# Weight blocks in fours, dots five gathers behind, and a yield between one-hots and their matmuls

## The chip, the cores and the metric

The kernel runs on one core of one Trainium2 chip. The metric is the time of one launch in microseconds on the device. Before the change three runs took 3744.71, 3747.1 and 3749.22 us; the median is 3747.1 us.

## What is computed

One layer of a decoder in float32 for two groups of rows: a prompt of 1024 rows (eight tiles of 128 rows, t = 0 to 7) and a sample group of 64 rows (tile 8, half a tile). Cut to what matters here:

```
h  = x @ w_in                                   # 1024 -> 3072, six chunks of 512 columns
a  = gelu(ua) * spatial_gate(gelu(va))          # two chunks
r  = silu(gr) * LN(retention(rot(q), rot(k), v))# four chunks, state carried from tile to tile
x1 = LN(ALPHA * x  + concat(a, r) @ w_o)
x2 = LN(ALPHA * x1 + attention(x1 @ ca_wq, mem_k, mem_v) @ ca_wo)
q  = x2 @ peer_wq                               # four chunks, 8 heads x 2 halves x 128
s  = q . subkeys;  top-16 per half -> 256 sums -> top-16 -> softmax weights g, expert numbers e
y  = LN(ALPHA * x2 + sum_e g_e * gelu(U[e] . x2) * V[e])     # 128 experts of 16384 per row
```

The results are y, the memory keys and values, the retention states and the normalised gate rows of the sample group.

## The kernel before

**Two streams.** Python generators emit the program: `main()` (the front, then the dense part) and `gathers()`. A loop at the end of `body` (L1154) advances the one whose clock is behind. Every `yield` names a cost, which is added to that stream's clock, and the clock is the due time (`tc.cur_priority`) of what is emitted next. Before the run a planner lays out each engine's queue: it walks through a modelled timeline and gives a free engine the earliest-due instruction that is ready in that model. On the chip each queue then runs strictly in that order, and an instruction whose input is late holds up all behind it.

**Front.** The tiles go through in four batches, [0], [1, 2, 8], [3, 4, 5], [6, 7]. `plan` lists chunks (a batch, a weight matrix and 512 of its columns): six of `w_in`, two each of `w_o`, `wq`, `wo`, and then four of `pq`, which for batches 1 and 2 are spread between the next batch's `w_in` chunks. A chunk has KB = 8 weight blocks of 128x512 (256 KB each), which SP loads in order into NR = 9 buffers (`Weights.load`, L136); a block's buffer is free once the last tile of the batch has used it. `Weights.mm` (L144) multiplies one tile by GK blocks in a row. The loop at L834 goes over KB / GK groups of blocks and, inside, over the tiles:

```
for grp in range(KB // GK):
    for t in tiles:
        ...
        yield from W.mm(i, grp, p[:P], lhs(key, t), lt)
        if grp < KB // GK - 1:
            step_all()
            continue
```

Each tile's sum is in one of three PSUM buffers (`mm`). After its last group, a tile's follow-up work (`post_gate`, `post_ret`, `post_att`, `post_res`, `post_peer`) joins the list `active`; each `step_all()` moves every entry one piece further. With the first chunk of `w_o`, `wq`, `wo` and `pq`, `drain(t)` first runs tile t's follow-up work to its end.

**Experts by gathers.** Tiles 0, 8, 5, 6 and 7 get their experts by indirect DMAs from the POOL queue: 576 gathers of 512 KB from U and as many from V into a ring of NG = 7 buffers (`gbuf`). `jobs` lists them in the order u0 v0 u8 v8 u5 v5 and so on. For each U gather `use` (L1062) emits one DVE instruction, the dot at L1071 with the rows of x2, due 15 units (DO) later than its place and put behind the DVE instruction emitted just before (`pin`). For each four V gathers PE does sixteen small matmuls (`cb`, L1104). A job is used LAG = 3 jobs after its gather is emitted. One job costs 1.1 units in the front; two weight blocks of a tile cost 1.3.

**Experts by tables.** Tiles 1 to 4 go through the dense part, which multiplies with all of U and V and needs a table of weights by expert. The end of `post_peer` builds it, one tile at a time (`gsl`): three transposes (L691), then for each of 32 groups g of four rows the one-hots (ACT at L702 and L703, DVE at L705), four matmuls (L719), an ACT copy into `big` (L720) and, for each four groups, a DMA to `gsc` (L723). One-hots for group g + 1 are emitted ahead of the matmuls of group g; the generator yields after every second group. The dense part waits for all four tables: `while st.get("gsl") or ...` (L988), and its own buffers open only when those of the tables are closed (L1000).

**Dense part.** 128 steps of `do_h` (L968) and of the V matmuls (L1024), with the rest of the gathers beside them.

Of the kernel before, what the change touches and what calls it, by code (L numbers as in the profile page):

```python
# [18 lines left out]
NT = 8  # L19
SMP = 8  # L20
KB = 8
GK = 2
ALPHA = 2.0 ** 0.25
EPS = 1e-5
GAM = [1.0 - 2.0 ** (-5.0 - h) for h in range(4)]
# [39 lines left out]
NG = 7  # L65
VQ = 4
LAG = 3
NFL = 3
ND = 2
GT = [0,8,5,6,7]  # L70
# [88 lines left out]
def body(ctx: ExitStack, tc: tile.TileContext, a):  # L159
    nc = tc.nc  # L160
# [94 lines left out]
    done = {}  # L255
# [332 lines left out]
    def post_peer(t, c, p, sub):  # L588
        P = rows(t)
# [95 lines left out]
        if c == 3 and dn:  # L685
            while st.get("gsl") or not st.get("gok"):
                yield
            st["gsl"] = True
            tp = GB()
            for j, src in enumerate((eid[:, 0, :], eid[:, 1, :], gw)):  # L690
                nc.tensor.transpose(tp[:, j * 128:(j + 1) * 128], src, ident)  # L691
            kt = TQ([128, 5, 128], "kt", 1)
            tpv = tp[:, :384].rearrange("p (a b) -> p a b", a=3)
            nc.scalar.activation(kt[:, :3, :], tpv, AF.Copy)
            nc.scalar.activation(kt[:, 3:5, :], tpv[:, 1:3, :], AF.Copy, scale=-1.0)
            yield
            n = DT.index(t)

            def onehots(g):
                oj = TQ([128, 4, 128], "oj", OJ)  # L700
                for r in range(4 * g, 4 * g + 4):
                    nc.scalar.activation(oj[:, r % 4, :], iota, AF.Abs, bias=kt[:, 3, r:r + 1])  # L702
                    nc.scalar.activation(oj[:, r % 4, :], oj[:, r % 4, :], AF.Relu, bias=kt[:, 2, r:r + 1], scale=kt[:, 4, r:r + 1])  # L703
                oi = TQ([128, 4, 128], "oi", OI)
                x = nc.vector.tensor_tensor(oi, iota.unsqueeze(1).to_broadcast([128, 4, 128]),  # L705
                                            kt[:, 0, 4 * g:4 * g + 4].unsqueeze(2).to_broadcast([128, 4, 128]), op=ALU.is_equal)
                pin(x, PO)
                return oi, oj

            nxt = onehots(0)  # L710
            for g in range(32):
                if g % 4 == 0:
                    gs = TQ([128, 128, 16], "big")
                oi, oj = nxt
                if g < 31:
                    nxt = onehots(g + 1)
                g4 = GB()
                for r in range(4):
                    nc.tensor.matmul(g4[:, r * 128:(r + 1) * 128], lhsT=oj[:, r, :], rhs=oi[:, r, :], start=True, stop=True)  # L719
                nc.scalar.activation(gs[:, :, g % 4 * 4:g % 4 * 4 + 4].rearrange("p i t -> p t i"),  # L720
                                     g4.rearrange("p (t i) -> p t i", t=4), AF.Copy)
                if g % 4 == 3:
                    nc.sync.dma_start(gsc[8 * n + g // 4], gs)  # L723
                if g % 2:
                    yield
            st["gsl"] = False
        elif c == 3:
            tp = GB() if XG else SM()
            nc.tensor.transpose(tp[:, :P], eid[:P, 0, :], ident[:P, :P])
            nc.vector.tensor_copy(done["ixT", t][:, :P], tp[:, :P])  # L730
            done["v", t] = True
            if t == SMP:
                for x in (done["ix", t], gw):
                    nc.sync.dma_start(x[64:, :64], x[:64, 64:])
                done["u", t, 3] = True
# [57 lines left out]
    def front():  # L793
        for i, (bi, name, c) in enumerate(plan):
# [39 lines left out]
            for grp in range(KB // GK):  # L834
                for t in tiles:
# [9 lines left out]
                        ps[t] = MM()  # L845
                    p = ps[t]
                    lt = t == tiles[-1]
                    yield from W.mm(i, grp, p[:P], lhs(key, t), lt)
                    if grp < KB // GK - 1:
                        step_all()  # L850
                        continue
                    del ps[t]
                    if c == NCH[name] - 1 and name != "wk":
# [196 lines left out]
    def gathers():  # L1050
# [75 lines left out]
                    nc.sync.dma_start(lb, bc(a["ln3_b"], 1024))  # L1126
                    finish(y, t, lg, lb)

        for m in range(len(jobs) + LAG):
            if m < len(jobs):  # L1130
                kind, t, i = jobs[m]
                P = rows(t)
                need = ("v", t) if kind == "v" else ("u", t, 3 if t == SMP else i // 32)
                while need not in done:
                    yield None
                if kind == "u" and i == 0:
                    x2s[t] = TG([128, 1024], "x2g", 1)
                    for j in range(0, 128, P):
                        nc.sync.dma_start(x2s[t][j:j + P], done["x2", t])
                g = TG([128, 1024], "gbuf", NG)  # L1140
                bufs[m] = g
                if kind == "u":
                    nc.gpsimd.indirect_dma_start(out=g, out_offset=None, in_=a["U"],  # L1143
                                                 in_offset=bass.IndirectOffsetOnAxis(ap=done["ix", t][:, i:i + 1], axis=0))
                else:
                    nc.gpsimd.indirect_dma_start(out=g, out_offset=None, in_=a["V"],  # L1146
                                                 in_offset=bass.IndirectOffsetOnAxis(ap=done["ixT", t][:, i:i + 1], axis=0))
            if m >= LAG:
                use(m - LAG)
            yield COST_F if phase[0] == 0 else COST_G  # L1150

    clocks = {"f": 0.0, "g": 0.0}
# [74 lines left out]
```

## Time and profile before

| | |
|---|---|
| runs | 3744.71, 3747.1, 3749.22 us; median 3747.1 |
| profiled execution | 3735.99 us, span 3734.1 us |
| PE | 3311.8 us busy (89%), mean granted clock 0.930 |
| DVE / ACT / POOL | 2331.6 (62%) / 1284.7 (34%) / 1573.6 us (42%) |
| DMA | 1039.72 MB, mean 278 GB/s |

All numbers come from one profiled execution. "Busy" is the time in which an engine ran an instruction; the granted clock is a share of TensorE's full 2.4 GHz. A float32 matmul of the program stands as two records in the trace. Idle time before an instruction is put down to the engine or DMA that released it.

### The profile page before, as it was taken

What the parts mean: (1) busy time and instruction counts of PE and PEld (TensorE: products, weight loads), DVE (VectorE), ACT (ScalarE), POOL (GpSimd) and SP (SyncE); (2) the same over time, 40 slices, a digit from 0 to 9 for tenths busy, and PEclk for the clock granted to TensorE, in tenths of its full rate; (3) what the DMA queues carried; (4) which work ended last, traced back from release to release, by engine and by line L of the source; (5) the groups of instructions that cost most, each with busy time, mean ns of one, the idle gap of its engine ahead of it and who ended that gap; (6) DMA issues with size and microseconds to landing.
All of it is one profiled execution on the core that took longest, in us unless ns stands there. A gap on an engine that the chain in (4) does not pass through costs nothing.

```text
span 3734.1 us, 42405 instructions
## 1 busy us (share of the span) xinstructions
PE 3311.8 (89%) x13881; PEld 2052.1 (55%) x13881; DVE 2331.6 (62%) x5894; ACT 1284.7 (34%) x2642; POOL 1573.6 (42%) x1363
## 2 busy tenths in 40 slices
PE   8999467889987999955888699999999999999998
PEld 3443223333445554432544477777777777666786
DVE  2135873225778523899759488788777777544556
ACT  1121211112258884222778722222222222222222
POOL 0013674244547532456645355454455544434100
PEclk9989688889988999977998799999999999999999
DMA  8757578677769886757988799999999999888632
GB/s 279 241 171 263 205 298 315 227 278 270 276 209 367 304 307 239 278 197 251 338 308 308 277 334 334 323 327 332 321 329 337 326 325 321 308 312 310 215 102 73
DMA packets 407356, 1039.72 MB, mean 278 GB/s; under 512 B 37280, under 2 KB 129632, under 8 KB 403040
## 3 DMA queue, kind: packets, MB, share of 16 engines
q0 software_dynamic: 165888, 604.05, 44.8%
q1 hardware_dynamic: 229392, 420.06, 32.9%
q10 hardware_dynamic: 11856, 12.91, 1.0%
q8 instruction: 109, 1.79, 0.2%
q14 instruction: 111, 0.91, 0.1%
HBM read 985.59 MB, written 51.25 MB: 278 GB/s over the span
## 4 chain that ended last, share of the span: by engine, by line
PE 63%; DVE 13%; DMA 11%; issue 5%; POOL 4%; ACT 4%; SPq 0%; POOLq 0%; ACTq 0%; DVEq 0%
PE mm L148 19%; PE h L973 15%; PE cb L1104 6%; PE oa L1024 4%; PE ob L1024 4%; PE oc L1024 4%; PE od L1024 4%; DVE gbuf L1071 4%; DMA gbuf<-in_V_dram,ixT 4%; DMA gbuf<-in_U_dram,ix 3%; PE gb L719 2%; POOL gbuf L1143 2%; DMA ret<-in_cv_dram 1%; PE sm L296 1%; POOL gbuf L1146 1%
## 5 line engine op out<-in xcount | busy, mean ns | idle before, releaser
L148 PE MATMUL mm<-wr,aT 128*128 128x512 f32 (+1 forms) x2432 | 1125.6, 610 | 31.1 <-DMA aT<-in_xpT_dram 17.9
L1146 POOL DMA_INDIRECT gbuf<-in_V_dram,ixT x576 | 619.0, 1075 | 838.5 <-PE cb L1104 495.5
L1143 POOL DMA_INDIRECT gbuf<-in_U_dram,ix x576 | 719.8, 1250 | 587.0 <-DVE hd L1071 349.1
L1071 DVE CUSTOM_DVE_ANT_0 gbuf<-gbuf,x2g 128x1024 f32<-128x1024 f32 x576 | 707.6, 1242 | 242.9 <-DMA gbuf<-in_U_dram,ix 199.0
L148 PEld LDWEIGHTS mm<-wr,aT 128*128 128x128 f32 (+1 forms) x2432 | 439.1, 190 | 583.3 <-issue 538.5
L973 PE MATMUL h<-x,uh 128*128 128x512 f32 x2048 | 644.2, 393 | 1.0 <-ACT uh L917 1.0
L973 PEld LDWEIGHTS h<-x,uh 128*128 128x128 f32 x2048 | 385.1, 189 | 105.4 <-issue 19.3
L973 PE MATMUL h<-x,ul 128*128 128x512 f32 x1024 | 402.1, 393 | 3.3 <-DVE ul L918 3.3
L1104 PE MATMUL cb<-gbuf,Z 128*32 128x512 f32 x2304 | 300.9, 621 | 25.7 <-DMA gbuf<-in_V_dram,ixT 25.7
L917 ACT ACTIVATE vh<-vr 128x1024 fp32r<-128x1024 f32 x128 | 135.5, 1061 | 546.0 <-PE od L1024 538.0
L719 PE MATMUL gb<-oi,oj 128*128 128x128 f32 x1024 | 170.7, 315 | 68.3 <-ACT big L720 37.5
L719 PEld LDWEIGHTS gb<-oi,oj 128*128 128x128 f32 x1024 | 153.2, 220 | 125.5 <-ACT oj L703 44.1
L973 PEld LDWEIGHTS h<-x,ul 128*128 128x128 f32 x1024 | 193.1, 189 | 52.3 <-issue 6.7
L918 DVE TENSOR_TENSOR ul<-ur,uh 128x1024 fp32r<-128x1024 f32 x128 | 156.5, 1222 | 95.4 <-ACT uh L917 95.1
L703 ACT ACTIVATE oj<-oj,kt 128x128 f32<-128x128 f32 x512 | 215.5, 485 | 0.0
L917 ACT ACTIVATE uh<-ur 128x1024 fp32r<-128x1024 f32 x128 | 135.4, 1059 | 231.2 <-PE h L973 227.3
L917 ACT ACTIVATE ah<-ga 128x512 fp32r<-128x512 f32 x128 | 80.8, 632 | 354.4 <-DVE ga L980 335.7
L705 DVE TENSOR_TENSOR oi<-cst,kt 128x512 f32<-128x512 f32 x128 | 88.9, 700 | 125.7 <-PE gb L719 124.4
L702 ACT ACTIVATE oj<-cst,kt 128x128 f32<-128x128 f32 x512 | 161.6, 391 | 14.8 <-PE gb L719 14.6
L660 POOL TENSOR_TENSOR cd<-cd,sif 128x512 f32<-128x512 f32 (+1 forms) x72 | 104.5, 1465 | 145.5 <-DVE cd L658 137.6
L1104 PEld LDWEIGHTS cb<-gbuf,Z 128*32 128x32 f32 x2304 | 62.5, 111 | 176.3 <-issue 138.4
L918 DVE TENSOR_TENSOR vl<-vr,vh 128x1024 fp32r<-128x1024 f32 x128 | 155.7, 1218 | 3.2 <-ACT vh L917 3.1
(228 smaller groups left out, 4796.7 us busy)
## 6 DMA issues: line engine op xcount, KB each, us to landing
ur<-in_Ud_dram SPq DMA_DIRECT2D x128, 512.0 KB, 6.6
vr<-in_V_dram SPq DMA_DIRECT2D x128, 512.0 KB, 5.8
wr<-in_w_in_dram SPq DMA_DIRECT2D x192, 256.0 KB, 5.3
wr<-in_pq_dram SPq DMA_DIRECT2D x128, 256.0 KB, 5.2
gsc<-big SPq DMA_DIRECT2D x32, 1024.0 KB, 6.8
G<-gsc SPq DMA_DIRECT2D x32, 1024.0 KB, 17.1
wr<-in_w_o_dram SPq DMA_DIRECT2D x64, 256.0 KB, 5.4
wr<-in_wq_dram SPq DMA_DIRECT2D x64, 256.0 KB, 7.4
```

What stands on the lines that cost most here:

```text
L148: self.nc.tensor.matmul(p, lhsT=lT(k), rhs=w, start=k == 0, stop=k == KB - 1)
L702: nc.scalar.activation(oj[:, r % 4, :], iota, AF.Abs, bias=kt[:, 3, r:r + 1])
L703: nc.scalar.activation(oj[:, r % 4, :], oj[:, r % 4, :], AF.Relu, bias=kt[:, 2, r:r + 1], scale=kt[:, 4, r:r + 1])
L719: nc.tensor.matmul(g4[:, r * 128:(r + 1) * 128], lhsT=oj[:, r, :], rhs=oi[:, r, :], start=True, stop=True)
L917: nc.scalar.activation(hi, raw, AF.Copy)
L918: nc.vector.tensor_tensor(lo, raw, hi.bitcast(F32), op=ALU.subtract)
L973: nc.tensor.matmul(p, lhsT=w[:, k, :], rhs=x[:, k, :], start=k == 0 and j == 0, stop=k == 7 and j == 2)
L1024: nc.tensor.matmul(o[j], lhsT=A[i][ia][:, n * 128:(n + 1) * 128], rhs=Vw[i][iv][:, j * 512:(j + 1) * 512], start=b == 0 and ia + iv == 0, ...
L1071: dot = nc.vector.tensor_tensor_reduce(out=g, in0=g, in1=x2s[t], scale=1.0, scalar=0.0, op0=ALU.mult, op1=ALU.add, accum_out=hd[t][:, i:i ...
L1104: nc.tensor.matmul(comb[t][q:q + 32, :], lhsT=Z[:, z + 4 * c1 + r1 % 4, 31 - r1:63 - r1], rhs=g1[:, n * 512:(n + 1) * 512], start=r1 == VQ ...
L1143: nc.gpsimd.indirect_dma_start(out=g, out_offset=None, in_=a["U"], in_offset=bass.IndirectOffsetOnAxis(ap=done["ix", t][:, i:i + 1], axis=0))
L1146: nc.gpsimd.indirect_dma_start(out=g, out_offset=None, in_=a["V"], in_offset=bass.IndirectOffsetOnAxis(ap=done["ixT", t][:, i:i + 1], axis=0))
```

## The change

GK goes from 2 to 4: a tile uses four blocks in a row, and a chunk has two groups instead of four. `step_all()` is still called after every two blocks except the last two of a chunk, so a chunk has as many as before. In `post_peer` the generator now yields in every group, between the one-hots of g + 1 and the matmuls of g: 32 yields instead of 16. In `gathers`, a U job is used five jobs behind (LAGU) while the stream is inside a run of U jobs with no V job pending and no final rows held; otherwise three behind as before. At the first U job of a tile all earlier jobs are used first. V jobs keep their lag. NG, NR and the work itself stay as they are.

```diff
-GK = 2
+GK = 4
+LAGU = 5
...
                 if g < 31:
                     nxt = onehots(g + 1)
+                yield
                 g4 = GB()
...
                 if g % 4 == 3:
                     nc.sync.dma_start(gsc[8 * n + g // 4], gs)
-                if g % 2:
-                    yield
...
-                    yield from W.mm(i, grp, p[:P], lhs(key, t), lt)
+                    for n, cost in enumerate(W.mm(i, grp, p[:P], lhs(key, t), lt)):
+                        yield cost
+                        if n < GK // 2 - 1 or grp < KB // GK - 1:
+                            step_all()
                     if grp < KB // GK - 1:
-                        step_all()
                         continue
...
-        for m in range(len(jobs) + LAG):
+        used = 0
+        for m in range(len(jobs) + 1):
...
                 if kind == "u" and i == 0:
+                    while used < m:
+                        use(used)
+                        used += 1
                     x2s[t] = TG([128, 1024], "x2g", 1)
...
+                del g
-            if m >= LAG:
-                use(m - LAG)
+            while used < m and (m == len(jobs) or m - used >= (LAGU if jobs[used][0] == kind == "u" and not pend and not fl else LAG)):
+                use(used)
+                used += 1
             yield COST_F if phase[0] == 0 else COST_G
```

## Rows read from the trace of the kernel before

**Rows 1.** Busy time by stretch of the span (start and end, length, then each engine's busy time with its instructions, the granted clock, the DMA share and GB/s).

```profile
0.00:300.00 300.00, 275.39 (x778) 130.24 (x779) 69.70 (x235) 56.14 (x120) 19.00 (x30) 0.95 0.70 230
300.00:600.00 300.00, 209.56 (x568) 92.50 (x566) 218.55 (x621) 51.38 (x121) 194.58 (x136) 0.79 0.73 267
600.00:1500.00 900.00, 796.31 (x3326) 392.02 (x3325) 451.52 (x1566) 399.14 (x982) 388.92 (x358) 0.92 0.78 276
1500.00:1760.00 260.00, 168.22 (x509) 88.83 (x508) 239.86 (x920) 61.97 (x162) 143.22 (x121) 0.79 0.70 243
1760.00:2130.00 370.00, 299.96 (x1391) 185.36 (x1391) 254.92 (x828) 289.77 (x726) 189.95 (x159) 0.87 0.85 307
2130.00:3734.00 1604.00, 1562.38 (x7314) 1163.18 (x7314) 1097.09 (x1726) 426.30 (x533) 637.97 (x560) 0.99 0.82 290
```

**Rows 2.** The timeline of PE in the front: start and length in us, line, tiles, count, and in brackets the idle time just before with what ended it.

```profile
440.91 0.34 PE L346 MATMUL sm<-cst,ret 64*128 64x64 f32 x1 [22.86 <-DVE ret L341]
...
482.48 0.66 PE L317 MATMUL sm<-g,wsS 64*64 64x128 f32 x2 [17.35 <-DVE g L309]
...
541.48 1.09 PE L296 MATMUL sm<-cst,nat 128*128 128x128 f32 x4 [9.88 <-DVE nat L459]
...
756.75 1.09 PE L296 MATMUL sm<-cst,nat 128*128 128x128 f32 x4 [4.04 <-DVE nat L459]
...
1220.49 0.96 PE L296 MATMUL sm<-cst,nat 128*128 128x128 f32 x4 [3.96 <-DVE nat L459]
...
1674.63 0.80 PE L364 MATMUL sm<-g 128*128 128x128 f32 x2 [16.75 <-ACT on L288]
...
1752.45 0.69 PE L691 MATMUL gb<-cst,eid 128*128 128x128 f32 x2 [26.07 <-DVE eid L664]
...
1896.65 1.94 PE L296 MATMUL sm<-cst,nat 128*128 128x128 f32 x8 [7.79 <-DVE nat L459]
```

**Rows 3.** The costliest groups of instructions: line, engine, operation, tiles, count, then busy us, mean ns of one, and the idle time before them.

```profile
L148 PE MATMUL mm<-wr,aT 128*128 128x512 f32 (+1 forms) x2432 | 1125.6, 610 | 31.1 <-DMA aT<-in_xpT_dram 17.9
...
L1071 DVE CUSTOM_DVE_ANT_0 gbuf<-gbuf,x2g 128x1024 f32<-128x1024 f32 x576 | 707.6, 1242 | 242.9 <-DMA gbuf<-in_U_dram,ix 199.0
...
L703 ACT ACTIVATE oj<-oj,kt 128x128 f32<-128x128 f32 x512 | 215.5, 485 | 0.0
...
L702 ACT ACTIVATE oj<-cst,kt 128x128 f32<-128x128 f32 x512 | 161.6, 391 | 14.8 <-PE gb L719 14.6
...
L720 ACT ACTIVATE big<-gb 128x512 f32<-128x512 f32 x128 | 130.6, 1045 | 47.2 <-PE gb L719 33.6 <-PE mm L148 7.0 <-DMA gsc<-big 6.3
```

**Rows 4.** A piece of the chain of waits: start, length, and a run of records without a gap.

```profile
1467.90 8.59 PE mm L148 x20
```

**Rows 5.** Two stretches of 50 us, columns as in rows 1.

```profile
350.00:400.00 50.00, 46.83 (x123) 19.41 (x122) 31.18 (x73) 7.98 (x18) 31.41 (x21) 0.83 0.72 243
...
1550.00:1600.00 50.00, 50.00 (x167) 26.19 (x166) 49.31 (x191) 12.44 (x31) 23.23 (x20) 1.00 0.92 342
```

**Rows 6.** From issue to landing: all loads of weight blocks (tile `wr`), and the U gathers (median, at the end of the row).

```profile
DMA to landing us min/median/max: 2.5/5.2/15.7
...
gbuf<-in_U_dram,ix POOLq DMA_INDIRECT x576, 7.2
```

**Rows 7.** Who waited for whom, DVE, in the stretches 280 to 580, 580 to 1540 and 1540 to 2130 us: total us, times, longest.

```profile
DVE gbuf L1071 <- DMA gbuf<-in_U_dram,ix: 39.3, 27, 8.2
...
DVE gbuf L1071 <- DMA gbuf<-in_U_dram,ix: 16.5, 17, 4.0
...
DVE gbuf L1071 <- DMA gbuf<-in_U_dram,ix: 23.4, 14, 5.6
```

**Rows 8.** The timelines of DVE and POOL around 519 us.

```profile
519.46 1.23 DVE L1071 CUSTOM_DVE_ANT_0 gbuf<-gbuf,x2g 128x1024 f32<-128x1024 f32 x1 [0.72 <-DMA gbuf<-in_U_dram,ix]
...
519.84 1.65 POOL L1143 DMA_INDIRECT gbuf<-in_U_dram,ix  x1 [0.30 <-issue]
521.80 1.66 POOL L1143 DMA_INDIRECT gbuf<-in_U_dram,ix  x1 [0.30 <-issue]
```

**Rows 9.** Who waited for whom, PE, in the stretches 1090 to 1540 and 1830 to 2130 us.

```profile
PE gb L719 <- ACT oj L703: 10.8, 11, 2.5
...
PE gb L719 <- ACT oj L703: 9.6, 11, 2.0
```

**Rows 10.** The timelines of ACT and PE where the third and the fourth table begin and the fourth ends.

```profile
1753.39 0.49 ACT L694 ACTIVATE kt<-gb 128x384 f32<-128x384 f32 x1 [2.63 <-PE gb L691]
...
1958.36 0.49 ACT L694 ACTIVATE kt<-gb 128x384 f32<-128x384 f32 x1
...
2124.97 0.47 PE L729 MATMUL gb<-cst,eid 128*128 128x128 f32 x1
```

**Rows 11.** Who waited for whom, POOL, in the stretches with U gathers in the front: 300 to 800, 1090 to 1300 and 1500 to 1900 us.

```profile
POOL gbuf L1143 <- DVE hd L1071: 112.6, 17, 52.0
...
POOL gbuf L1143 <- DVE hd L1071: 14.6, 11, 4.5
...
POOL gbuf L1143 <- DVE hd L1071: 20.7, 14, 3.1
```

More of the change, by code (lines that the diff above doesn't have):

```diff
@@ L1141, in gathers @@
                 bufs[m] = g
[L1142 to L1147, printed above, removed]
-            if m >= LAG:
-                use(m - LAG)
+                ap, src = (done["ix", t], "U") if kind == "u" else (done["ixT", t], "V")
+                nc.gpsimd.indirect_dma_start(out=g, out_offset=None, in_=a[src],
+                                             in_offset=bass.IndirectOffsetOnAxis(ap=ap[:, i:i + 1], axis=0))
+                del g
+            while used < m and (m == len(jobs) or m - used >= (LAGU if jobs[used][0] == kind == "u" and not pend and not fl else LAG)):
+                use(used)
+                used += 1
             yield COST_F if phase[0] == 0 else COST_G
```

## The prediction

> **What bounds the kernel now.** I read first the busy time by stretch [rows 1]. From 2130 us on PE is busy 1562 of 1604 us at a granted clock of 0.99: nothing in the change takes work from PE, so this part keeps its length and only moves with its start. Before 2130 us PE stands still 380 us: 25 to 300 us, then 90 of 300 us, 104 of 900, 92 of 260 and 70 of 370. In the second and the fourth of these stretches the granted clock is 0.79, and DVE is busy 219 of 300 and 240 of 260 us. These two hold nearly half of the idle time.
>
> Then I read what ends PE's long stalls [rows 2]. All but one end in something that DVE makes (rotated rows L341, gate rows L309, normalised rows L459, expert numbers L664), the other (L288) in an ACT step that needs DVE's statistics. They stand where a batch goes from `w_in` to `w_o`, from `w_o` to `wq`, and from `wo` to the transposes of x2: there all tiles' follow-up work has to be finished before PE goes on. In the last stretch of the front it is the tables: ACT is busy 290 of 370 us [rows 1], and the dense part waits for the fourth table, which begins at 1958 and ends at 2125 us [rows 10].
>
> So the time is the front's 2130 us, with its stalls on DVE and its tables on ACT, and a dense part that follows. The profiled execution took 3735.99 us, 1.9 us more than its span and 11 us below the median of 3747.1. The sum is made on it and carried over to the median.
>
> **Part 1, four blocks in a row.** The matmuls are the same. One call is two records, and 20 records in a row take 8.59 us [rows 4], so a call costs 0.86 us and the 1216 calls behind the 2432 records [rows 3] stay. What moves is the end of each tile within its chunk. With three tiles and two blocks in a row the tiles end 4, 2 and 0 calls before the chunk's end; with four in a row 8, 4 and 0. The first tile's follow-up work starts 4 calls or 3.44 us sooner, the second's 2 calls or 1.72 us; in a batch of two tiles the first's 1.72 us. By the chunk's end the first tile has also had five calls of `step_all` since its own end, not three, so that less is left to `drain`. The last tile's work starts where it did. Batch 0 has one tile: nothing changes there.
>
> Where does that reach the end? At four of the stalls [rows 2] PE waits for normalised rows, and in program order the first tile's come first: 9.88 us at 541, 4.04 at 757, 3.96 at 1220 (three tiles, 3.44 us each) and 7.79 at 1897 (two tiles, 1.72 us). Behind them the first tile then has four calls, not two, to cover the next tile's wait. That is 3 x 3.44 + 1.72 = 12.0 us. For the stalls of 22.86 and 17.35 us, which belong to one passage from `w_in` to `w_o`, I take 3.44 us once: shortly before, at 350 to 400, DVE is busy only 31 of 50 us [rows 5] and has room to start sooner. For the 16.75 and 26.07 us stalls I take nothing: at 1550 to 1600 DVE is busy 49.3 of 50 us [rows 5], so work that is ready sooner only queues sooner. Together 15.5 us. The bounds are nothing, and all eight stalls, 109 us.
>
> Against it stand the weight loads. A load is issued when the block nine places earlier is done with. Counted from the loop, the shortest time from there to its first use falls with three tiles from 20 calls to 16, 17.2 to 13.8 us, and with two tiles from 14 to 12, 12.0 to 10.3 us. Loads land after 5.2 us in the median and 15.7 at most [rows 6]: only the tail gets through. Now 31.1 us of idle time stand before the matmuls, 17.9 of them for `aT` and not weights [rows 3], so weights cost at most 13.2 us. I add 2 us; the bounds are 0 and a doubling, 13 us. SP's other transfers (x2g, `big`) queue behind a load that waits for its buffer, up to four calls or 3.4 us longer; that lies within the same bound.
>
> **Part 2, dots five behind.** The dots stay 576 at 1.24 us [rows 3]. A job costs 1.1 units, two blocks cost 1.3 units and 1.72 us, so a job is 1.46 us where PE runs freely, and a dot moves 2 jobs or 2.9 us later among DVE's work. Three jobs are 4.4 us, five are 7.3; a gather lands 7.2 us after its issue [rows 6]. Before 2130 us dots made DVE wait for their gather 39.3 + 16.5 + 23.4 = 79.2 us, 58 times [rows 7], 1.37 us each, which is less than the 2.9 us by which they move. What of it counts is the share that falls where PE stands still. By stretch that is 30% (300 to 600), 11.5% (600 to 1500) and 26% (1500 to 2130) [rows 1]: 11.8 + 1.9 + 6.0 = 19.7 us. I don't take it all, since the ring of seven is not longer: a gather still waits for the dot seven places earlier, so a stream that runs late stays late. I take two fifths, 8 us. The bounds are a gain of 19.7 us, and a loss, which is the slower rival below.
>
> One rule speaks against this part. Around 519 us each dot waits 0.72 us for its gather, while gathers of 1.65 us follow each other with 0.30 us between them and wait for no dot [rows 8]: the pace there is POOL's, not the ring's. The Trainium skill (Perfetto Trace Analysis, Identifying the Most-Contended Engine) says that the same gap repeating on an engine that should be saturated can mean there are too few buffers for the next tile. By this row the 8 us stand as they are; by that rule dots that hold their buffers longer lose where I let them gain, and the sum would be that of the slower rival.
>
> **Part 3, the yield.** The instructions are the same. In emission a table takes 32 pieces instead of 16, at one piece for each two blocks (1.72 us) 55 us instead of 28. In execution the fourth took 167 us [rows 10], 5.2 us a group, of which ACT's one-hots and copy alone are (215.5 + 161.6 + 130.6) / 128 = 4.0 us [rows 3]. The due times run far ahead of ACT either way, so tables keep their place ahead of later work and their pace, and from pq's end there are more than enough pieces before the dense part. I take 0. The bounds: PE waited 10.8 + 9.6 = 20.4 us for one-hots [rows 9], which is the most that distance can save; and one group more at the end of the third and the fourth table, 2 x 5.2 = 10.4 us, straight on the end, since the dense part waits for it.
>
> **Sum.** -15.5 + 2 - 8 + 0 = -21.5 us: 3714.5 us on the profiled execution, 3725.6 on the median. I predict 3726 us; this case's own range is 3705 to 3739.
>
> **Rivals.**
>
> *Hidden, 3745 us.* DVE has a fixed amount to do at the passages, and work that starts sooner moves the wait to the next item. For it: 240 of 260 us busy from 1500 on [rows 1]. Against it: the room at 350 to 400 [rows 5], and four stalls behind normalised rows where the chain's length counts. It includes that the dots don't really come later, because not the lag but the ring sets when they run.
>
> *The ring turns against POOL, slower.* Seven buffers with dots five behind leave a gather two places of slack, not four. POOL runs in order, and behind a gather that waits for a dot stand the small powers (L283), the products (L660) and the halves of the normalisation (L458, L459) that DVE and PE wait for. POOL waited for a dot in the front 17 + 11 + 14 = 42 times, 148 us [rows 11]. Each 2.9 us longer is 123 us; in the stretches where PE stood still a third of the time (182 of 560 us [rows 1]) that makes 40 us. Less part 1's 13.5 us it is +26 us: 3773 us. For it: rows 11. Against it: much of that waiting (52 us once) has nothing urgent behind it. It decides from 42 us more on POOL's waits for dots, where its third eats up part 1.
>
> *The passages close up, 3674 us.* If first tiles really run ahead, DVE's load spreads, and a third of the 182 us of idle time at the two passages goes, with the 12 us elsewhere: -73 us. For it: the clock of 0.79 there [rows 1], so that shorter stalls also give back slow matmuls. Against it: DVE's 92% from 1500 to 1760.
>
> **How the numbers follow.** The forecast gets 0.45, hidden 0.18, slower 0.23, closing up 0.14. Faster by over 0.2% (7.5 us, about what a measurement of this kernel tells from no change) is the forecast and closing up, 0.59; within it the hidden case, 0.18; slower 0.23. The range is 3680 to 3772: below it half of the last case, above it somewhat under half of the slower one. Such a range has to be wide because the planner lays out all queues anew, and a different order among equal claims can cost or give as much as a term of the sum.
>
> **What would show it.** Right: before the first tile's transposes at the passages the waits for L459 are some 3 us shorter; DVE's waits for U gathers in the front fall from 79 us by a third or more; the fourth table still takes about 167 us and everything from it to the end about 1609. Part 1 is wrong if these waits stay or PE waits for `wr` more than 13 us. Part 2 is wrong if the waits for gathers stay, and the slower rival is right if POOL's waits for dots rise above 190 us. Part 3 is wrong if a table's time or its end moves apart from its start by more than 10 us. The forecast as a whole is wrong if the span after the fourth table changes, or if the front does not get shorter by 14 us or more.

## The result, and the profile after

The changed kernel takes 3768.8 us in the median of six runs; the kernel before, beside it on the same chip, 3746.8. The ratio is 1.0061, 95% interval 1.0044 to 1.0079: 22 us slower, where 21 us faster was predicted. The figure lies inside the predicted range, at its upper edge.

The profiled execution has a span of 3763.6 us, 29.5 more than before. Busy time by stretch, in the stretches and columns of [rows 1]:

```profile
0.00:300.00 300.00, 275.39 (x778) 129.71 (x779) 70.44 (x235) 55.63 (x120) 18.94 (x30) 0.96 0.70 230
300.00:600.00 300.00, 204.02 (x563) 90.18 (x562) 213.35 (x615) 49.49 (x116) 196.59 (x134) 0.80 0.72 259
600.00:1500.00 900.00, 772.54 (x3247) 383.67 (x3247) 435.28 (x1456) 394.37 (x968) 378.82 (x357) 0.92 0.77 276
1500.00:1760.00 260.00, 192.64 (x580) 101.73 (x578) 229.35 (x978) 63.20 (x162) 125.20 (x104) 0.83 0.65 223
1760.00:2130.00 370.00, 282.77 (x1316) 172.15 (x1317) 273.23 (x866) 270.63 (x675) 202.88 (x170) 0.87 0.83 304
2130.00:3763.00 1633.00, 1579.87 (x7402) 1177.57 (x7400) 1109.14 (x1746) 458.50 (x608) 650.07 (x570) 0.98 0.82 291
```

PE did 24 us less between 600 and 1500 us, 17 less between 1760 and 2130, and 24 more between 1500 and 1760: the front runs late. PE's stalls, as in [rows 2] (most lines stand one higher here, so L460 is the L459 of before):

```profile
396.27 1.26 PE L609 MATMUL sm<-sub,pqT 128*128 128x128 f32 x8 [4.45 <-DMA sub<-in_subT_dram]
...
435.69 0.34 PE L347 MATMUL sm<-cst,ret 64*128 64x64 f32 x1 [19.82 <-DVE ret L342]
...
469.82 0.48 PE L729 MATMUL gb<-cst,eid 128*128 128x128 f32 x1 [15.35 <-DVE eid L667]
...
481.62 0.66 PE L318 MATMUL sm<-g,wsS 64*64 64x128 f32 x2 [11.32 <-DVE g L310]
...
537.73 1.09 PE L297 MATMUL sm<-cst,nat 128*128 128x128 f32 x4 [8.05 <-DVE nat L460]
...
568.86 0.69 PE L297 MATMUL sm<-cst,nat 64*128 64x64 f32 x4 [8.60 <-POOL nat L460]
...
1125.51 0.36 PE L729 MATMUL gb<-cst,eid 64*128 64x64 f32 x1 [12.01 <-DVE eid L667]
...
1230.79 1.09 PE L297 MATMUL sm<-cst,nat 128*128 128x128 f32 x4 [4.09 <-DVE nat L460]
...
1786.97 1.08 PE L297 MATMUL sm<-cst,nat 128*128 128x128 f32 x4 [31.73 <-DVE nat L460]
...
2043.77 2.08 PE L609 MATMUL sm<-sub,pqT 128*128 128x128 f32 x8 [7.40 <-DMA sub<-in_subT_dram]
```

In batch 1's passage from `w_in` to `w_o` two stalls are shorter (22.86 to 19.82 and 17.35 to 11.32 us), and 15.35 us at 470 have come in between. Also new are 12.01 us at 1126 and 11.9 us for sub-keys; the long stall just ahead of the third table, 26.07 us, is 31.73. The 8.60 us behind POOL at 569 are not new, only longer; in the kernel before:

```profile
565.32 0.69 PE L296 MATMUL sm<-cst,nat 64*128 64x64 f32 x4 [5.50 <-POOL nat L459]
```

ACT shows where the third and the fourth table begin and where the last copy of the fourth is:

```profile
1789.42 0.49 ACT L695 ACTIVATE kt<-gb 128x384 f32<-128x384 f32 x1 [0.72 <-PE gb L692]
...
1990.21 0.48 ACT L695 ACTIVATE kt<-gb 128x384 f32<-128x384 f32 x1
...
2160.68 2.14 ACT L722 ACTIVATE big<-gb 128x512 f32<-128x512 f32 x2
```

Against [rows 10] the third table starts 36.0 us late and the fourth 31.9; from the fourth's last copy to the end it is 1600.8 us, 7.3 less than before. DVE's waits for U gathers, in the stretches of [rows 7]:

```profile
DVE gbuf L1073 <- DMA gbuf<-in_U_dram,ix: 37.5, 25, 8.7
...
DVE gbuf L1073 <- DMA gbuf<-in_U_dram,ix: 29.9, 30, 4.8
...
DVE gbuf L1073 <- DMA gbuf<-in_U_dram,ix: 24.6, 20, 5.4
```

Together 92.0 us, not less than the 79.2 of before. POOL's waits for dots, in the stretches of [rows 11]:

```profile
POOL gbuf L1149 <- DVE hd L1073: 127.3, 22, 25.7
...
POOL gbuf L1149 <- DVE hd L1073: 24.7, 20, 4.0
...
POOL gbuf L1149 <- DVE hd L1073: 23.5, 14, 7.2
```

These are 175.5 us in 56 waits. They can't be set beside the 147.9 us in 42 waits of [rows 11]: in the changed kernel one line issues the gathers from U and from V, and of its waits 165.6 us in 46 stand before gathers from U. In the kernel before the gathers from V have a line of their own, without such a wait in the first stretch, and in the other two:

```profile
POOL gbuf L1146 <- DVE hd L1071: 6.7, 2, 6.1
...
POOL gbuf L1146 <- DVE hd L1071: 4.7, 4, 2.7
```

So it is 165.6 us for 147.9 before gathers from U, and 175.5 for 159.3 in all.

### The profile page after: what moved, and what is told of

It reads as the page before. It is cut to its first block, busy times and chain, and to the rows that moved or that the text cites. A ratio compares the mean times of both kernels' runs of the same rounds, so it can differ in the third digit from the quotient of the medians.

```text
span 3763.6 us, 42375 instructions
## 1 busy us (share of the span) xinstructions
PE 3307.2 (88%) x13881; PEld 2055.0 (55%) x13881; DVE 2330.8 (62%) x5894; ACT 1291.8 (34%) x2648; POOL 1572.5 (42%) x1363
## 4 chain that ended last, share of the span: by engine, by line
PE 62%; DMA 11%; DVE 11%; issue 6%; ACT 5%; POOL 4%; SPq 0%; POOLq 0%; DVEq 0%; ACTq 0%
PE mm L149 18%; PE h L975 15%; PE cb L1106 6%; DMA gbuf<-in_V_dram,ixT 5%; PE oa L1026 4%; PE oc L1026 4%; PE ob L1026 4%; PE od L1026 4%; DVE gbuf L1073 3%; POOL gbuf L1149 3%; DMA gbuf<-in_U_dram,ix 3%; PE gb L721 2%; ACT oj L704 1%; ACT oj L703 1%; ACT big L722 1%
## 5 line engine op out<-in xcount | busy, mean ns | idle before, releaser
L1149 POOL DMA_INDIRECT gbuf<-in_U_dram,ix x576 | 737.0, 1280 | 600.3 <-DVE hd L1073 367.2
L1149 POOL DMA_INDIRECT gbuf<-in_V_dram,ixT x576 | 603.2, 1047 | 809.2 <-PE cb L1106 500.6
L920 DVE TENSOR_TENSOR ul<-ur,uh 128x1024 fp32r<-128x1024 f32 x128 | 158.7, 1240 | 93.1 <-ACT uh L919 92.8
L703 ACT ACTIVATE oj<-cst,kt 128x128 f32<-128x128 f32 x512 | 163.7, 391 | 17.8 <-PE gb L721 17.7
```

What stands on the lines that cost most here:

```text
L920: nc.vector.tensor_tensor(lo, raw, hi.bitcast(F32), op=ALU.subtract)
L1149: nc.gpsimd.indirect_dma_start(out=g, out_offset=None, in_=a[src], in_offset=bass.IndirectOffsetOnAxis(ap=ap[:, i:i + 1], axis=0))
```

## The experiments

All ratios are to the kernel before on the same chip; the half-widths of their intervals (in brackets) are 0.12 to 0.28 percentage points, called points below; 0.1 point is about 4 us. A trace is one execution, and executions of the kernel before lie between 3725 and 3760 us, so a difference of some 10 us between the spans of two traces says little. The edits, taken singly and together, are these. **Blocks** is GK = 4 with its loop, **yield** the moved `yield`, as in the change. The gather loop's part is cut in two: the **lag** of five for dots, and the **flush**, which uses up all pending jobs before a new token block begins:

```
                 if kind == "u" and i == 0:
+                    while used < m:
+                        use(used)
+                        used += 1
                     x2s[t] = TG([128, 1024], "x2g", 1)
```

Without the flush and with a lag of three, the rewritten loop gives the order of before in every queue, instruction for instruction. The **control** edit gives the planner's clock another cost for one gather job and changes nothing else:

```
-COST_F = 1.1
+COST_F = 1.12      (or 1.08)
```

### The parts alone

e1, the blocks:

> The four blocks in a row alone. Theory A (the blocks cost: bursts of weight loads hold up what queues behind them on SP, first of all the sub-key loads, and the passages gain nothing): 10 to 25 us slower than before, with a wait of PE for `sub` of some us as in the changed kernel. Theory B (the dots five behind cost, the blocks gain a little as predicted): 5 to 15 us faster. Theory C (the yield costs): within 8 us of before. Theory D (each edit lays the queues out anew and the differences are of that size whatever the edit means): anything within 25 us, with no one wait that carries it.

Measured: 3709.1 us, ratio 0.992 [0.9902, 0.9938]: 33 us faster by the medians, 30 by the ratio, more than any of the theories allowed.

e2, flush and lag:

> The dots five behind alone. Theory A: within 8 us of before. Theory B (the rival of the ring: buffers held longer, POOL waits longer for dots, DVE's waits for gathers don't fall): 10 to 30 us slower, POOL's waits for dots in the front well over 148 us. Theory C: within 8 us. Theory D: anything within 25 us, and then the same loop with the old lag of three moves by as much.

Measured: 3757.8 us, 1.0035 [1.0023, 1.0048]: 13 us slower, in the range of theory B. But POOL's waits for dots, which theory B wanted well over 148 us, are 152.0 before gathers from U, counted as above; theory D's range holds it too.

e3, the yield:

> The yield alone. Theory A and theory B: within 8 us of before. Theory C (table one-hots come sooner in program order, take ACT and the g4 buffers where the front's own work wants them, and the tables last longer, 172 for 167 us): 10 to 25 us slower, the first table's stretch from w_in to w_o of batch 2 some 16 us longer than in the kernel before, as in the changed kernel. Theory D: anything within 25 us.

Measured: 3742.3 us, 1.0005 [0.9992, 1.0017]: no difference. In this trace w_in5 to w_o of batch 2 takes 81.9 us, as before.

e4, the flush with the old lag:

> The rewritten gather loop with the old lag of three for U as well, so that only the flush ahead of a new token block and the order in the loop differ. Theories A, B and C: within 5 us of before. Theory D: it moves by 8 us or more either way although no dot comes later.

Measured: 3763.3 us, 1.0052 [1.0034, 1.007]. No dot comes later, and it costs no less than e2, as theory D has it. The trace shows what the flush does. SP, POOL and DVE in the kernel before, where token block 0 ends and block 8 begins:

```profile
1111.28 0.34 SPq L1125 DMA_DIRECT2D gbuf<-in_ln_g_dram  x1
...
1083.40 0.94 POOL L1146 DMA_INDIRECT gbuf<-in_V_dram,ixT  x1 [0.30 <-issue]
1112.00 1.02 POOL L1143 DMA_INDIRECT gbuf<-in_U_dram,ix  x1 [4.72 <-DMA ix<-ix]
...
1120.41 1.21 DVE L899 TENSOR_TENSOR gbuf<-gbuf 128x1024 f32<-128x1024 f32 x1
```

The same with the flush (e4):

```profile
1093.91 0.33 SPq L1126 DMA_DIRECT2D gbuf<-in_ln_g_dram  x1
...
1095.06 0.94 POOL L1148 DMA_INDIRECT gbuf<-in_V_dram,ixT  x1 [0.30 <-issue]
1130.36 1.17 POOL L1148 DMA_INDIRECT gbuf<-in_U_dram,ix  x1 [9.23 <-PE gb L720]
...
1124.75 1.22 DVE L900 TENSOR_TENSOR gbuf<-gbuf 128x1024 f32<-128x1024 f32 x1
```

The rows of block 0 are now finished ahead of block 8's first gather. Their loads of `ln3` are issued before the last V gather and hold two of the seven buffers from there, and the first U gather comes 35.3 us after the last V gather, not 28.6. Batch 2 goes from w_in5 to w_o meanwhile: 99.1 us for 82.7.

No theory explained all of this: the blocks alone gain more than predicted, no other part costs as much, and the whole loses. So the parts were paired.

### The parts in pairs

e5, lag without flush:

> Dots five behind in the old order of the loop: the flush of pending jobs ahead of a new token block is left out, four blocks and yield are as before. Theory F (the flush costs: it finishes the block before ahead of the new block's gathers, at its end in batch 2's passage from w_in to w_o; the lag itself is worth little): within 8 us of the kernel before, with the gathers of token block 8 starting some 18 us sooner than with the flush. Theory G (buffers held longer cost, the rival of the ring): 10 to 25 us slower, as with the flush. Theory N (any new order of the queues is worth up to 20 us): anything.

Measured: 3756.3 us, 1.0046 [1.0025, 1.0067]. Block 8's first gather follows the last V gather after 28.5 us, as before, and the time is still as with the flush: theory G. DVE's waits for gathers, counted as above, are 92.6 us.

e6, blocks and lag:

> Four blocks in a row and dots five behind, no flush, no yield. Theory F: both keep their worth, 25 to 40 us faster than before, as with the four blocks alone. Theory G: the four blocks lose 15 us or more of their 33. Theory N: anything between the changed kernel and 40 us faster.

Measured: 3755.0 us, 1.0041 [1.0025, 1.0057]. The blocks lose all of their 33 us and 15 more.

e7, blocks and flush:

> Four blocks in a row and the rewritten loop with its flush, dots three behind. Theory F: the flush takes some 20 us from the 33 that the four blocks gave, so 8 to 18 us faster than before. Theory G: as with the four blocks alone, 25 to 40 us faster, since no dot comes later. Theory N: anything.

Measured: 3732.3 us, 0.9975 [0.9961, 0.9989]: 9 us faster, as theory F has it.

e8, blocks and yield:

> Four blocks in a row and the yield, the gather loop as before. Theories F and G: the yield stays without effect, 25 to 40 us faster than before. Theory H (with four blocks in a row step_all is called at other places, and one-hots a group ahead at the new places take from the passages what the blocks gave): 10 us faster or less.

Measured: 3737.3 us, 0.9981 [0.9968, 0.9993]: 7 us faster, as theory H has it, though the yield alone did nothing.

e9, the change without the flush:

> The changed kernel with only the flush left out. Theory F (the flush costs by itself, 21 us in the loop with the old lag, 24 on the four blocks): 3745 us or less, with batch 2's passage from w_in to w_o some 15 us shorter than in the changed kernel. Theory G (dots five behind undo the four blocks, as in the kernel with both and no flush): within 10 us of that kernel's 3755. Theory N: anything within 25 us of the changed kernel.

Measured: 3754.7 us, 1.0033 [1.0019, 1.0047]. As theory G has it. Batch 2's passage is 92.8 us, 6 less than in the changed kernel, not 15.

e10, the change without the yield:

> The changed kernel with only the yield put back as it was. Theories F and G: within 8 us of the changed kernel's 3768. Theory H (the yield undoes the four blocks, as it took 28 us from them in the pair): 15 to 30 us faster than the changed kernel. Theory N: anything between.

Measured: 3736.7 us, 0.9989 [0.9974, 1.0004]: 0.72 points or 27 us better than the changed kernel, as theory H has it; but between e6 and e9 the same yield makes no difference. Whichever part goes last into a good kernel seems to cost 20 to 45 us. That asks for the controls.

### Controls: the same edits, another order

In the trace of e11 some 5,100 of PE's 13,881 records stand at another place than in the kernel before, and none is added.

e11, the kernel before at 1.12, and e17 at 1.08:

> A control: the kernel before, with a job's cost in the planner's clock 1.12 instead of 1.10, so that no instruction is added, dropped or asked for at another distance, but the order of a third of the instructions shifts a little. Theories F, G and H: within 5 us of before. Theory N (order alone is worth up to 20 us): 8 us or more away on either side.

> The kernel before with a job's cost of 1.08. Theory N: anywhere from 15 us faster to 20 us slower than at 1.10; if the scatter belongs to four blocks in a row alone, within 5 us, as at 1.12.

Measured: 3735.5 us, 0.9987 [0.9973, 1.0001], and 3731.4 us, 0.9972 [0.9961, 0.9984]. At 1.12 that is 5 us, within what F, G and H allow and short of theory N's 8; at 1.08 it is 10 us, as only theory N has it.

e12 and e18, the blocks alone at 1.12 and 1.08:

> The same control on the four blocks alone. If the 33 us are the four blocks' own: within 8 us of their 3709. Theory N (the 3709 is one good order among others): 3720 us or more.

> The four blocks alone with a job's cost of 1.08. If the blocks have an effect of their own of the size predicted (13 us and some), it lies below the kernel before at 1.08 by 5 to 25 us, wherever that lies; theory N alone: as likely above as below it.

Measured: 3733.5 us, 0.9976 [0.9959, 0.9992], and 3742.5 us, 1.0005 [0.9993, 1.0017]. At 1.08 the blocks are 0.33 points above the kernel before, not below it: a miss for their having the predicted effect in every order.

e13 and e14, the changed kernel at 1.12 and 1.08:

> The changed kernel with a job's cost in the planner's clock 1.12 instead of 1.10. If the 22 us are the change's own: within 8 us of 3768. Theory N (order): 3755 us or less, or 3780 or more.

> The same with 1.08. If the 22 us are the change's own: within 8 us of 3768. Theory N: 3755 us or less, or 3780 or more, and not where 1.12 lies.

Measured: 3754.9 us, 1.0012 [0.9999, 1.0026], and 3742.2 us, 0.9986 [0.9972, 1.0]. Theory N's case, twice. The three settings together:

```
job cost          1.08     1.10     1.12     mean
before           0.9972   1        0.9987   0.9986
blocks           1.0005   0.992    0.9976   0.9967
whole change     0.9986   1.0061   1.0012   1.0020
```

A step of 2% in a number that adds no work moves the blocks by 0.85 points (32 us) and the change by 0.75 (28 us). Most of e1's 33 us is a lucky order, and of the changed kernel's 22 us some 9 are an unlucky one: over the three orders the change costs 0.34 points, 13 us, and the blocks give 0.19, 7 us. With rows that spread by 0.3 to 0.85 points, three orders do not make either mean certain.

### Where the orders differ

In each trace the third table starts once the expert numbers of its tokens are there, the fourth when the third has ended, and the dense part follows. All in us; the first three columns are the starts of chunks (batch 1's second `wq`, batch 2's last `w_in` and first `w_o`), then the third table's start, the length of the third and of the fourth (to its last copy), the rest, and the span:

```
kernel                       b1 wq1  b2 w_in5  b2 w_o0  third at  third  fourth  rest    span
before                        578.7    1065.0   1147.7   1753.4   205.0  167.7  1608.1  3734.1
e11 before, 1.12              575.3    1058.0   1142.8   1752.1   202.3  166.1  1603.5  3724.0
e17 before, 1.08              577.8    1061.9   1147.6   1738.8   219.3  166.6  1600.9  3725.6
e3  yield                     582.3    1073.4   1155.3   1757.6   228.6  152.1  1604.6  3742.9
e4  flush                     583.8    1076.7   1175.8   1778.8   218.2  165.1  1599.9  3761.9
e5  lag                       584.1    1069.3   1155.9   1753.3   220.8  168.9  1609.8  3752.9
e2  flush, lag                582.6    1075.7   1179.0   1776.3   225.5  155.2  1600.0  3757.0
e1  blocks                    564.5    1051.8   1138.0   1745.1   177.8  175.7  1606.8  3705.5
e12 blocks, 1.12              566.8    1049.2   1141.8   1761.4   193.4  167.1  1601.4  3723.4
e18 blocks, 1.08              570.3    1062.6   1152.9   1786.5   184.1  163.7  1604.3  3738.6
e8  blocks, yield             570.1    1056.9   1143.5   1734.5   221.9  175.6  1607.9  3739.8
e7  blocks, flush             567.4    1055.1   1146.4   1769.6   187.5  169.9  1601.9  3728.9
e6  blocks, lag               581.5    1064.2   1157.2   1753.0   191.3  196.1  1612.9  3753.2
e10 blocks, flush, lag        582.0    1070.7   1168.3   1763.9   190.4  179.1  1607.3  3740.7
e9  blocks, lag, yield        578.4    1064.1   1156.9   1758.1   214.9  172.1  1610.4  3755.4
the change                    579.7    1066.4   1165.3   1789.4   200.8  172.6  1600.8  3763.6
e13 the change, 1.12          569.7    1062.6   1162.2   1769.6   223.5  157.7  1608.0  3758.9
e14 the change, 1.08          574.2    1067.1   1150.7   1754.5   222.6  158.5  1607.0  3742.7
```

The rest is 1600 to 1613 us everywhere. So a span is set by the start of the third table (1734 to 1789) and by the two tables (348 to 397 us), and these do not go together: e8 has the earliest third table and the longest pair. What makes the third long can be read off PE. Its projection matmuls between the starts of the two tables, in the shortest of these tables (e1):

```profile
L148 PE MATMUL mm<-wr,aT 128*128 128x512 f32 x170 | 80.8, 618 | 2.6 <-ACT aT L411 2.6
```

and in the longest (e3):

```profile
L148 PE MATMUL mm<-wr,aT 128*128 128x512 f32 x239 | 116.5, 628 | 7.7 <-DMA wr<-in_wo_dram 5.8 <-ACT aT L411 1.9
```

The planner queued 69 records more, 36 us, between one-hot matmuls of the same table. They then do not stand in the fourth (152.1 for 175.7 us). Over all 18 kernels of the list the count goes with the third table's length (correlation 0.81), not strictly. In 15 of the 18 it is the same 256 records, shared out between the two tables.

Two kernels that differ in one part alone make a pair. The pairs are, for the blocks, e1, e12 and e18 to the kernel before at the same job cost, e8 to e3, e7 to e4, e6 to e5 and e10 to e2; for the lag e5 to before, e6 to e1, e2 to e4, e10 to e7 and e9 to e8; for the flush e4 to before, e7 to e1, e2 to e5, e10 to e6 and the change to e9; for the yield e3 to before, e8 to e1, e9 to e6 and the change to e10. The means of their differences, in us of the list above, and for the ratio in points of the measured times:

```
part      third at    third   fourth     rest    ratio   pairs
blocks       +0.5     -24.7    +12.2     +2.2    -0.30     7
lag          +4.6      +6.5     +3.5     +3.1    +0.43     5
flush       +23.0      +2.5     -7.7     -7.6    +0.14     5
yield        +6.1     +25.4    -11.6     -2.9    +0.33     4
```

Three of these have one sign in every pair. With the blocks the third table is shorter, by 6.7 to 35.2 us; with the yield it is longer, by 10.4 to 44.1; with the flush it starts later, by 10.9 to 31.3. The first two go with the queue: the blocks take 7 to 88 projection records out of the third table, the yield puts 33 to 79 in. The length of the third table also keeps the blocks and the kernel before apart at each of the three job costs (178 to 193 us for 202 to 219). The measured ratio has one sign throughout for none of the four parts, and all pairs but two of the blocks' have a job cost of 1.10.

e15 and e16 test the path itself: the one-hots' second pass is left out of two tables, so those tables hold other numbers.

```
-nc.scalar.activation(oj[:, r % 4, :], oj[:, r % 4, :], AF.Relu, ...)
+if n < 2:          (e15; n >= 2 in e16)
+    nc.scalar.activation(oj[:, r % 4, :], oj[:, r % 4, :], AF.Relu, ...)
```

> The kernel before without the second pass of the one-hots (the Relu) in the third and the fourth table, so these tables hold other numbers; 256 passes of 0.32 us, 81 us of ACT, are left out. Theory T (the front ends with tables three and four one behind the other on ACT): both tables together 40 to 80 us shorter and the whole 40 to 80 us faster. If the passages' stalls of PE set the end and tables fill gaps: less than 15 us faster.

> The same 81 us of ACT left out of the first and the second table instead. Theory T: these two tables end 40 us or more sooner, but the third starts where it did (it waits for the expert numbers of its tokens) and the whole is within 15 us of before. If ACT's work counts wherever it is: 40 us faster or more.

Measured: e15 3720.3 us, 0.993 [0.9902, 0.9957], 26 us faster, short of what was expected (and the pass left out is the one at L703, 215.5 / 512 = 0.42 us each [rows 3], so more than the 81 us was left out); e16 3765.8 us, 1.0042 [1.0028, 1.0057], 16 us slower. The stretches of the third and the fourth table, columns as in [rows 1], in the kernel before:

```profile
1753.00:1958.00 205.00, 172.20 (x760) 103.82 (x759) 137.27 (x357) 149.15 (x377) 111.41 (x92) 0.91 0.87 317
1958.00:2126.00 168.00, 129.75 (x643) 83.10 (x641) 124.36 (x481) 147.14 (x368) 84.89 (x73) 0.82 0.81 290
```

and in e15:

```profile
1756.00:1958.00 202.00, 173.31 (x769) 106.02 (x769) 148.88 (x417) 104.17 (x256) 107.85 (x89) 0.91 0.87 314
1958.00:2099.00 141.00, 108.88 (x624) 72.71 (x627) 109.94 (x413) 95.55 (x231) 78.15 (x67) 0.87 0.88 320
```

ACT does 45 us less in the third table, and the table is 3 us shorter: so ACT does not set its pace. PE, 172 to 173 us busy in both, is the likelier; no run takes work from PE alone. In the fourth ACT does 52 us less and 27 come out. So theory T holds for the fourth table, where ACT is busy 147 of 168 us, and fails for the third. The 26 us by themselves would lie within what another order does, but 141 us for the fourth table lie below the 152 to 196 of all 18 kernels of the list. In e16 the second table shrinks from 174 to 145 us and ends 32 us sooner, not 40, but the third starts 7 us later, not earlier, and lasts 232 us instead of 205: nothing of the saving arrives, and the time is one us outside the 15 that were allowed.

## Why the prediction was wrong

**Part 1 (15.5 us less, 2 back).** The size came out near, by another way, and that is luck. In seven pairs of kernels that differ in the blocks alone, the difference is -0.30 points or 11 us in the mean, for 13.5 forecast, and it runs from -0.80 (e1) to +0.33 (e18). Two of the priced stalls moved as worked out: before the first tile's transposes at 541 us PE waits 10.7 us in the mean of the five kernels with dots three behind and without the blocks, and 6.5 in the five with them; at 757 it is 3.9 and 1.1, at 1220 4.1 and 4.1. What failed is the step from there to the end. In the means of the same two fives, by starts of chunks, the kernels with the blocks lead by 11.6 us where batch 1 starts its last `w_in`, ahead of all passages that the working named (360 to 369 us in all kernels with the blocks, 375 to 380 in all without). They lead by 5.6 at `w_o` and 11.8 at the second `wq`, are 4.9 behind at batch 2's first `w_in`, lead by 11.9 at its last, and are 3.3 behind where the third table starts. So the lead in the first two columns of the list is not what arrives. The gain at the end comes from the third table's length, 24.7 us less in the mean of the seven pairs, which no term of the working moves. In batch 1's passage from its last `w_in` to `w_o` the hidden rival was right: PE is idle 63.2 us there before and 65.7 in e1, whose stalls read

```profile
432.48 0.34 PE L346 MATMUL sm<-cst,ret 64*128 64x64 f32 x1 [21.52 <-DVE ret L341]
...
465.76 0.47 PE L729 MATMUL gb<-cst,eid 128*128 128x128 f32 x1 [15.54 <-DVE eid L666]
476.40 0.66 PE L317 MATMUL sm<-g,wsS 64*64 64x128 f32 x2 [10.16 <-DVE g L309]
...
531.90 2.15 PE L296 MATMUL sm<-cst,nat 128*128 128x128 f32 x8 [6.47 <-DVE nat L459]
```

DVE ends each of the first three, and what one loses another gains. The last is the stall of 9.88 us of [rows 2], 3.4 us shorter, for the term of 3.44 us. The cost side was small as worked out: PE waits 3.9 us for `wr` in the changed kernel; the 11.9 us for sub-keys came on top (0.8 in e1), which the working did not name among SP's other transfers.

**Part 2 (8 us less).** Wrong in sign. In five pairs that differ in the lag alone it costs 0.43 points or 16 us in the mean, from -0.17 (e4 to e2) to +1.21 (e1 to e6). The two fifths of DVE's waits for gathers were not there to be taken: in these pairs the waits change by +13.4, +5.0, -2.5, -14.5 and +0.6 us, 0.4 in the mean, where the test asked for a third less. The 92.0 us of the changed kernel are not the lag's alone: e5, the lag alone, has 92.6, but e4, with the flush and dots three behind, has 92.3. The working's own doubt, that the ring is not longer, so that a stream that runs late stays late, fits this; no run has a longer ring, so that it is the cause is not shown. The rule weighed there, that a repeated gap can mean too few buffers (the Trainium skill, Perfetto Trace Analysis, has it in the section Optimization Strategy), has the sign right for the time, and shows no more than that. The slower rival has the sign too, not the price: POOL's waits for dots grow in all five pairs, by 1.0 to 28.0 us, 13.8 in the mean, and before gathers from U they are 165.6 us in the changed kernel, under the 190 named. Part of what five behind costs shows at batch 1's second `wq`: with the blocks it starts at 577.6 us in the mean of six kernels for 567.8 with three behind. The 8.60 us stall behind POOL at 569 lies just ahead of it in the changed kernel, as in e6, e9 and e10; in e13 and e14 it is 2.3 and 3.5.

The working has nothing on the flush: it read the change as later dots only, though the diff shows the loop over pending jobs. In all five pairs the flush lengthens batch 2's passage from w_in5 to w_o, by 16.4 and 16.7 us without the blocks and 5 to 6 with them, and the third table starts 23 us later in the mean. At the end little of that is left: 0.5 points in two pairs (e4, e7), 0.28 in the changed kernel against e9, and -0.11 and -0.52 in the two others.

**Part 3 (0).** The time is as forecast for the yield alone (e3) and between e6 and e9; it is 0.61 and 0.72 points slower between e1 and e8, and e10 and the change, 0.33 points or 12 us in the mean of the four. The step that failed is that tables keep their pace. By this part's own test of 10 us the yield moves the third table in all four pairs (23.6, 44.1, 23.6 and 10.4 us longer), and the fourth is 6.5 to 24.0 us shorter in three. The working had a table's emission stretched from 28 to 55 us and let the due times swallow it; the queues show 33 to 79 more projection records between the starts of the two tables. e8 and e1 reach batch 2's `wo` within 3 us of each other, and e8's third table even starts 11 us sooner, but then takes 44 us longer. In the changed kernel itself the blocks hide it: its third table is 4.2 us shorter than before. Its fourth takes 172.6 us and the rest 1600.8, as the test of this part asked.

**The sum.** The first failure lies under all three: the terms of 2 to 15 us were added as if the rest stood still, while a 2% step of a planner's cost alone moves these kernels by 5 to 32 us. The prediction did say that a different order can cost as much as a term; it used that for the range only, not for the chances of the sign. By the means of the pairs the blocks give 0.30 points where 13.5 us (0.36) were forecast, the lag costs 0.43 where 8 us (0.21) were to be gained, and the yield and the flush, both at nothing in the sum, cost 0.33 and 0.14. That adds up to 0.60, and 0.61 was measured; it is an account, not a proof, since the pairs share kernels and scatter as widely as the means are large. The second is the place where the end is decided. The prediction took PE's stalls as the currency and the fourth table as a fixed piece; the spans are the third table's start (just ahead of it PE waits 26.07 us on DVE before and 31.73 in the change), and the third and the fourth table one behind the other, whose sum, 348 to 397 us, was not taken as something that the change moves. Of the changed kernel's 29.5 us of span, 36.0 are the late start; the tables give back 4.2 and cost 4.9, and the rest gives 7.3. Of the 36.0, 17.6 are there at batch 2's `w_o` (1.4 at its last `w_in`, so 16.2 arise in the passage between), 5.3 come until that batch's last `pq` chunk, and 13.1 from there to the table. The same kernel without the flush (e9) starts the third table 4.7 us later than before, so at this job cost 31.3 of the 36.0 come with the flush, 6.1 of them in that passage; without it the two tables are 13.6 us longer and the rest 9.6, so that the end moves by 8 us only. The change's three orders start the third table at 1789, 1770 and 1755 us. How an order turns into one or the other stays open; so does whether the blocks' 7 us, or the change's 13, would hold over more orders.

The fastest kernel measured is e1, the blocks alone at a job cost of 1.10: 3709.1 us, 0.8% below the kernel before.

## What to carry to other kernels

Where a planner lays out the queues, time each edit at two or three settings of something that adds no work before believing a gain or a loss: here the spread was up to 0.85%, more than any single part was worth in the mean. Look for the pieces that stand one behind the other up to the end (here a start, two tables, a rest) and ask of each edit which of them it moves. And read a diff for the waits that bookkeeping brings, such as using up what is pending, not only for the number that it changes.

## What was not expected of the hardware

The same operation on POOL, half of a normalisation for 64 rows, takes 1.28 us in e1, while DVE runs nothing,

```profile
555.11 1.28 POOL L459 TENSOR_TENSOR nat<-nat,lng 64x512 f32<-64x512 f32 x1
```

and 9.60 us in the changed kernel:

```profile
559.21 9.60 POOL L460 TENSOR_TENSOR nat<-nat,lng 64x512 f32<-64x512 f32 x1
```

In these 9.60 us DVE runs seven dots without a gap, the first from 559.61, the last to 567.69 (rows of the changed kernel):

```profile
559.61 1.21 DVE L1073 CUSTOM_DVE_ANT_0 gbuf<-gbuf,x2g 128x1024 f32<-128x1024 f32 x1
...
566.48 1.21 DVE L1073 CUSTOM_DVE_ANT_0 gbuf<-gbuf,x2g 128x1024 f32<-128x1024 f32 x1
```

POOL gets through only when the run ends, and PE waits 8.60 us for it. The kernel before has the same case at 555.7 us (9.61 us, and PE waits 5.50). The Trainium skill (SBUF — State Buffer, Who interferes with whom) says that a VectorE instruction with two inputs in SBUF contends with a GpSimd instruction that reads SBUF, and calls the shared ports an exclusive lock; that whoever issues first holds them for its whole instruction it says there of VectorE's 2-port modes. The trace agrees that POOL does not get through beside the dots, and adds that it is not let in between seven of them that follow each other every 1.15 us. So in these two cases a run of dots that had piled up, each of them ready, cost POOL's next step the length of the run.
